# Seven-product SwiGLU with context: the w2 product behind two block products, A12 loaded twice, two block sums made by accumulating transfers

## The chip, the core and the metric

The kernel runs on one core of a Trainium2 chip. The metric is the device time of one execution in microseconds (us). A core has a matrix engine (TensorE, PE in the profile), a vector engine (VectorE, DVE), a scalar engine (ScalarE, ACT), GpSimd (POOL) and a queue that issues transfers (SyncE, SP). Matmuls read SBUF and write PSUM; weights and activations that don't fit in SBUF are fetched from device memory (HBM) by transfers (DMA).

## What is computed

A backbone of two layers over 512 latent tokens `x` and 256 context tokens `ctx`, width 1024. Each layer is half-step SwiGLU, token mixing, half-step SwiGLU; every sub-layer is normalised and modulated by shift, scale and gate vectors that a large matrix product (`w_ada`, 9 times 1024 columns per layer) makes of a conditioning vector. The context goes through the same weights, except for the last SwiGLU.

```python
def swiglu(x, w1, w3, w2):
    return (jax.nn.silu(x @ w1) * (x @ w3)) @ w2

def macaron_half(h, m, i, g, w1, w3, w2):
    y = swiglu(modulate(rms_norm(h, g), m[:, 3 * i], m[:, 3 * i + 1]), w1, w3, w2)
    return h + 0.5 * m[:, 3 * i + 2, None, :] * y
```

`w1` and `w3` have 2816 columns, 22 blocks of 128. Everything is float32.

## The kernel before, in words

Activations are kept transposed: `self.h` is eight tiles of 128 x 768 (256 context and 512 latent columns). A float32 product is made of three matmuls (`mm3`, L396 to L398): each operand is split into a high and a low part, the high part by ACT (L403, or L406 with a factor), the low part by a subtraction on DVE (L404, or L407), and high x high, high x low and low x high are summed in PSUM. So a block of weights passes through a tile `raw` (as loaded by SP, five such tiles) and a tile `w` (split, four such tiles), 128 x 1024 each: 512 KB.

Of the four SwiGLUs, the first of layer 0 is plain. The other three go through `ffn7`, which treats the hidden blocks in 11 pairs and saves one of eight block products: with the weights of a pair as blocks A11, A12, A21, A22 it makes seven products of sums of A blocks with sums of activation blocks. Two of these three carry the context too. In the trace of before, the first of them (the second SwiGLU of layer 0, **stage A** below) lies from 1045 to 1530 us, the other (the first SwiGLU of layer 1, **stage B**) from 1595 to 2080 us; the last SwiGLU of layer 1, for `x` alone, is the end of the program.

The first pair of an `ffn7` is plain (`first_pair`); `combine` makes the sums of activation blocks after it, and `pair(j, middle)` runs for each later pair. In `pair`, the products are B11 into PSUM bank Y, B21 into X, E into Y, t3 into X, t1 into Y, t4 into X, B22 into Y, each of 8 `mm3`, 24 matmuls of 384 columns. `snapshot` (L888) copies a bank to a tile `y` by ACT; `gated` (first line L894) adds a bank to such a copy on DVE and makes the gated hidden values of it. `middle()` is the w2 product of the pair before: for 8 blocks of rows of `h` and both streams, two hidden blocks into a bank B (6 matmuls of 512 columns for `x`, 6 of 256 for the context), and an accumulation into `h` on DVE (L905). It comes behind B11. The sums of weight blocks are three DVE additions of 128 x 1024, L973 (A21 + A22), L974 (A11 + A21) and L975 (A11 + the first), and L977 updates A12.

The modulation vectors are made beside all this: `self.mod_queue` holds pieces of work, each a load of a block of `w_ada` and two custom DVE instructions (L483), and `mods` says how many of them are taken behind which pair.

The order of instructions on each engine is not the order of this code: a list scheduler arranges it when the kernel is built, under the limits of the tiles (five `raw`, four `w`, 44 others).

Of the kernel before, what the change touches and what calls it, by code (L numbers as in the profile page):

```python
# [312 lines left out]
class Builder:  # L313
# [315 lines left out]
    def ffn(self, l, i, n, gate, nxt, streams=(X_COLS, C_COLS), begin=None, mods=0, split=None):  # L629

        nc = self.nc
        w13, w2 = self.a["w13"][l], self.a["w2"][l, i]
# [167 lines left out]

    def split_block(self, r, scale=None):
        w = self.mp.tile([128, 2, 1024], F32R, tag="w", name=self.name("w"), bufs=self.wslots)
        self.split_psum(w[:, 0], w[:, 1], r, scale)
        return w

    def ffn7(self, l, i, n, t, gate, nxt, streams=(X_COLS, C_COLS), split=None, late=None, mods=()):
# [12 lines left out]
        mp13, w2 = self.a["w13s"][2 * l + i - 1], self.a["w2"][l, i]  # L819
# [11 lines left out]
        def combine(k):  # L831

            u, v = t[k], t[k + 4]
            tensor = nc.vector.tensor_tensor
            tensor(out=u[:, n1], in0=u[:, n1], in1=u[:, n2], op=ALU.subtract)
            tensor(out=u[:, n2], in0=v[:, n2], in1=u[:, n2], op=ALU.subtract)
            tensor(out=v[:, n2], in0=u[:, n1], in1=v[:, n2], op=ALU.add)
            tensor(out=v[:, n1], in0=v[:, n2], in1=v[:, n1], op=ALU.subtract)
            c = slice(halves[0][0], halves[1][1])
            hi, lo = self.hl(T, "c")  # L840
            self.split_psum(hi[:, c], lo[:, c], v[:, c])
            tt[k, "t4"], tt[k, "E"] = ([p[:, q] for p in (hi, lo)] for q in (n1, n2))
            owned.append((hi, lo))
            if k % 2 == 0:
                box["t3"] = self.hl(2 * wd, "c")
                owned.append(box["t3"])
            tt[k, "t3"] = [p[:, k % 2 * wd:k % 2 * wd + wd] for p in box["t3"]]
            self.split_psum(*tt[k, "t3"], u[:, n2])
            self.free(t.pop(k + 4))

        def combine_rest():

            for k in range(4):
                tt[k, "t1"] = [p[:, n2] for p in n[k]]
                self.split_psum(*tt[k, "t1"], t[k][:, n1])
                self.free(t.pop(k))
# [41 lines left out]
        def down(fs, ws, d, cols):  # L898
# [3 lines left out]
            for x, f in enumerate(fs):  # L902
                self.mm3(ps[:, 0:c1 - c0], [ws[x][:, p, d * 128:d * 128 + 128] for p in range(2)],
                         (g[f][0][:, c0:c1], g[f][1][:, c0:c1]), x == 0, x == len(fs) - 1)
# [48 lines left out]
        def second(j):  # L953
            return [self.unit(w2[f]) for f in (2 * j, 2 * j + 1)]

        def pair(j, middle):
# [3 lines left out]
            Y, X = (self.ps("S", (j + x) % 2) for x in range(2))  # L960
            r11 = self.block(src[0, 0])
            product(Y, self.split_block(r11), "B11", True)
            middle()
            y0 = snapshot(Y, "y")
            gtiles(j)
            s = [self.m3(base="silu") for _ in range(2)]
            r12 = self.block(src[0, 1])
            product(X, self.split_block(r12), "B21", True)
            r21, r22, s1 = self.block(src[1, 0]), self.block(src[1, 1]), self.block(None)
            gated(s[0], n1, X, y0, 1.0)  # L970
            self.free(y0[0])
            parts(fs[0], s[0], n1)
            add(s1, r21, r22)  # L973
            add(r21, r11, r21)  # L974
            add(r11, s1, r11)  # L975
            product(Y, self.split_block(r11, -1.0), "E", False)
            add(r12, r11, r12)  # L977
            y1 = snapshot(Y, "y")
            product(X, self.split_block(r21), "t3", True)
            w0 = snapshot(X, "y")  # L980
            if j == 1:
                combine_rest()
            product(Y, self.split_block(s1), "t1", False)
            gated(s[1], n2, Y, w0, -1.0)
            self.free(w0[0])
            product(X, self.split_block(r22), "t4", False)
            if j == np_ - 1:
                self.free(owned)
# [3 lines left out]
            product(Y, self.split_block(r12), "B22", False)  # L992
            self.last_silu = nc.scalar.activation(s[0][:, n2], Y[:, 0:wd], AF.Silu)
# [6 lines left out]
        for k in range(4):  # L1000
            combine(k)
# [913 lines left out]
```

## Time and profile before

| what | value |
|---|---|
| median of 3 runs | 2764.53 us (2761.27 to 2767.53) |
| the profiled execution, own time | 2769.52 us |
| its span in the trace | 2767.7 us |
| granted TensorE clock, mean | 0.984 |
| PE, DVE, ACT, POOL busy | 96%, 74%, 39%, 10% of the span |
| mean share of the 16 DMA engines, q1 | 27.6% |

The profiled execution is 5.0 us longer than the median. An execution's own time is 1.8 us longer than its span, for what lies around it. The granted clock is the share of TensorE's full clock that the chip allowed; 0.50 means that matmuls started half as often.

### The profile page before, as it was taken

How to read it: one execution, taken by the hardware profiler on the slowest of the kernel's cores; microseconds unless marked ns; L12 is line 12 of the kernel's file. 1: busy time of each engine (PE TensorE's matmuls, PEld its weight loads, DVE VectorE, ACT ScalarE, POOL GpSimd, SP SyncE). 2: the span in 40 equal slices, each digit the busy share in tenths (PEclk: the TensorE clock that was granted, in tenths of full speed). 3: DMA queues.
4: the chain of work that ended last, by engine and by line, in shares of the span. 5: the costliest groups of instructions: out<-in, count | busy, mean ns of one | idle time of the engine just before them, and what ended most of it. 6: DMA issues, size and time to landing. Idle time of an engine off the chain costs nothing.

```text
span 2767.7 us, 40029 instructions
## 1 busy us (share of the span) xinstructions
PE 2658.0 (96%) x15788; PEld 2357.8 (85%) x15788; DVE 2046.8 (74%) x3551; ACT 1087.9 (39%) x1895; POOL 278.8 (10%) x370
## 2 busy tenths in 40 slices
PE   7999999999989998999999989999999989999999
PEld 5788888888867788999899879999998877888998
DVE  8986776655775559778676799887756675587886
ACT  4311211124665653233232632323335665544443
POOL 5100000001352210000000100000001352100000
PEclk8899999999989999999999999999999999999999
DMA  7542433211200013233222244443222210123322
GB/s 246 162 136 94 158 117 113 83 54 56 75 22 24 12 46 111 90 102 99 81 75 69 67 125 128 141 144 121 84 76 67 69 32 24 39 80 106 98 93 91
DMA packets 78673, 249.60 MB, mean 90 GB/s; under 512 B 8978, under 2 KB 10642, under 8 KB 78484
## 3 DMA queue, kind: packets, MB, share of 16 engines
q1 hardware_dynamic: 78484, 247.03, 27.6%
q8 instruction: 124, 2.03, 0.3%
q14 instruction: 65, 0.53, 0.1%
HBM read 244.90 MB, written 2.10 MB: 89 GB/s over the span
## 4 chain that ended last, share of the span: by engine, by line
PE 78%; DVE 14%; ACT 3%; issue 3%; DMA 2%; POOL 0%; SPq 0%; DVEq 0%; ACTq 0%; POOLq 0%
PE S L396 14%; PE S L398 13%; PE S L397 13%; PE B L397 10%; PE B L398 10%; PE B L396 10%; PE B L1424 3%; DVE w L404 2%; DVE junk L483 2%; PE B L1575 2%; DVE h L905 1%; DMA raw<-in_w13s 1%; DMA ada<-in_w_ada 1%; ACT w L403 1%; PE B L1543 1%
## 5 line engine op out<-in xcount | busy, mean ns | idle before, releaser
L403 ACT CAST w<-raw 128x1024 fp32r<-128x1024 f32 (+1 forms) x369 | 381.3, 1044 | 723.3 <-issue 330.0
L397 PE MATMUL S<-nlo,w 128*128 128x256 f32 (+2 forms) x1808 | 598.0, 331 | 9.4 <-DVE nlo L605 6.2
L396 PE MATMUL S<-nhi,w 128*128 128x256 f32 (+2 forms) x1808 | 590.0, 332 | 12.7 <-DVE silu L994 4.3
L398 PE MATMUL S<-nhi,w 128*128 128x256 f32 (+2 forms) x1808 | 596.4, 331 | 2.7 <-DVE w L404 2.5
L404 DVE TENSOR_TENSOR w<-raw,w 128x1024 fp32r<-128x1024 f32 (+1 forms) x369 | 449.2, 1229 | 95.3 <-ACT w L403 94.2
L397 PE MATMUL B<-glo,w 128*128 128x512 f32 (+1 forms) x1232 | 425.4, 346 | 5.6 <-DVE glo L870 5.6
L398 PE MATMUL B<-ghi,w 128*128 128x512 f32 (+1 forms) x1232 | 423.0, 346 | 3.1 <-DVE w L404 3.1
L396 PE MATMUL B<-ghi,w 128*128 128x512 f32 (+1 forms) x1232 | 416.2, 348 | 6.4 <-DVE h L905 2.7
L905 DVE SCALAR_TENSOR_TENSOR h<-B,g,h 128x512 f32<-128x512 f32 (+1 forms) x440 | 273.3, 642 | 145.5 <-PE B L398 144.7
L397 PEld LDWEIGHTS S<-nlo,w 128*128 128x128 f32 x1808 | 343.6, 190 | 33.8 <-DVE nlo L605 10.5
L396 PEld LDWEIGHTS S<-nhi,w 128*128 128x128 f32 x1808 | 341.4, 190 | 35.7 <-DVE silu L994 4.3
L398 PEld LDWEIGHTS S<-nhi,w 128*128 128x128 f32 x1808 | 344.2, 190 | 25.8 <-DVE w L404 6.9
L397 PEld LDWEIGHTS B<-glo,w 128*128 128x128 f32 x1232 | 232.0, 188 | 35.5 <-DVE glo L870 6.5
L396 PEld LDWEIGHTS B<-ghi,w 128*128 128x128 f32 x1232 | 229.8, 188 | 37.8 <-DVE h L905 5.1
L483 DVE CUSTOM_DVE_ANT_0 junk<-ada,bc,mpart 128x768 f32<-128x768 f32 x238 | 245.6, 1032 | 20.3 <-DMA ada<-in_w_ada 16.9
L398 PEld LDWEIGHTS B<-ghi,w 128*128 128x128 f32 x1232 | 231.7, 188 | 33.8 <-DVE w L404 3.8
L396 PE MATMUL S<-chi,w 128*128 128x384 f32 (+1 forms) x720 | 232.1, 323 | 13.5 <-ACT y L888 10.7
L398 PE MATMUL S<-chi,w 128*128 128x384 f32 (+1 forms) x720 | 229.1, 321 | 2.7 <-DVE w L404 2.1
L397 PE MATMUL S<-clo,w 128*128 128x384 f32 (+1 forms) x720 | 230.5, 321 | 0.0
L691 DVE SCALAR_TENSOR_TENSOR h<-B,g,h 128x256 f32<-128x256 f32 (+1 forms) x176 | 103.8, 615 | 101.6 <-PE B L398 101.6
L532 POOL TENSOR_TENSOR sq<-sq,sq 128x512 f32<-128x512 f32 (+1 forms) x38 | 42.2, 1112 | 1159.3 <-ACT sq L528 1158.1
L888 ACT COPY y<-S 128x768 f32<-128x768 f32 (+1 forms) x90 | 65.5, 728 | 237.7 <-PE S L398 130.9
(267 smaller groups left out, 4413.6 us busy)
## 6 DMA issues: line engine op xcount, KB each, us to landing
raw<-in_w SPq DMA_DIRECT2D x132, 512.0 KB, 3.6
raw<-in_w13s SPq DMA_DIRECT2D x132, 512.0 KB, 3.8
ada<-in_w_ada SPq DMA_DIRECT2D x171, 384.0 KB, 4.0
raw<-in_w_out SPq DMA_DIRECT2D x16, 512.0 KB, 4.3
ada<-in_ada SPq DMA_DIRECT2D x16, 384.0 KB, 6.4
raw<-in_w_in_t SPq DMA_DIRECT2D x10, 512.0 KB, 3.5
raw<-in_dftx SPq DMA_DIRECT2D x8, 512.0 KB, 3.5
ada<-in_ada SPq DMA_DIRECT2D x8, 256.0 KB, 5.2
```

Source lines behind the costliest of these rows:

```text
L396: mm(out, lhs[0], rhs[0], start=start, stop=False, skip_group_check=more)
L397: mm(out, lhs[0], rhs[1], start=False, stop=False, skip_group_check=more)
L398: mm(out, lhs[1], rhs[0], start=False, stop=stop, skip_group_check=more)
L403: nc.scalar.copy(hi, src)
L404: nc.vector.tensor_sub(lo, src, hi.bitcast(F32))
L483: nc.vector.tensor_tensor_reduce(out=self.junk[:, 0:w.shape[1]], in0=w, in1=v, scale=1.0, scalar=init, op0=ALU.mult, op1=ALU.add, accum_ou ...
L532: (nc.vector if part else nc.gpsimd).tensor_add(st[key], st[key], t)
L691: nc.vector.scalar_tensor_tensor(out=self.h[d][:, c0:c1], in0=ps[:, 0:c1 - c0], scalar=gate()[:, d, s:s + 1], in1=self.h[d][:, c0:c1], op0 ...
L888: nc.scalar.copy(v, both(bank))
L905: nc.vector.scalar_tensor_tensor(out=self.h[d][:, c0:c1], in0=ps[:, 0:c1 - c0], scalar=gate()[:, d, s:s + 1], in1=self.h[d][:, c0:c1], op0 ...
L1424: mm(outs[y], lhs[y], rhs[y], start=start, stop=stop)
L1575: nc.tensor.transpose(pt[:, x * 256 + i * 128:x * 256 + i * 128 + 128], Ps[i, y][:, tok(kp * 2 + x)], self.ident)
```

## The change

For the two SwiGLUs with context (not for the last one), five things are different.

1. `middle()` stands behind B11, B21 and the first `gated`, and no longer between B11 and B21.
2. w2 is packed anew: a half-unit holds both hidden blocks of a pair for 512 columns, and each half is loaded and split when its first use comes.
3. A21 + A22 and A11 + A21 are made by transfers (`block_sum`): SP loads the first block into a `raw` tile, and a second transfer, issued by POOL (L805), reads the other block from HBM and adds it to that tile. The two DVE additions are gone. As A11 + A21 no longer overwrites A21 nor uses the loaded A11, and since A12 and A22 are fetched where they are used, A12 is loaded twice. In 20 pairs this is 2 more SP loads and 2 POOL transfers each: SP's transfers go from 548 to 588 rows, POOL's rows from 325 to 365, DVE's from 3552 to 3517. PE has 15035 rows in both.
4. `combine` runs in three parts within the first of these pairs, ahead of the product that needs each, and no longer whole ahead of it.
5. The pieces of the modulation begin two pairs later.

The core of the diff:

```diff
+    def block_sum(self, *srcs):
+        r = self.block(srcs[0])
+        for src in srcs[1:]:
+            self.nc.gpsimd.dma_start(out=r, in_=src, accum_op=ALU.add)
+        return r
...
         def pair(j, middle):
...
+            first = combine if j == 1 else lambda name: None
             r11 = self.block(src[0, 0])
             product(Y, self.split_block(r11), "B11", True)
-            middle()
+            if x_only:
+                middle()
             y0 = snapshot(Y, "y")
...
             r12 = self.block(src[0, 1])
             product(X, self.split_block(r12), "B21", True)
...
             gated(s[0], n1, X, y0, 1.0)
             self.free(y0[0])
+            if not x_only:
+                middle()
+                gtiles(j)
             parts(fs[0], s[0], n1)
-            add(s1, r21, r22)
-            add(r21, r11, r21)
+            if x_only:
...
+            else:
+                s1, s3 = self.block_sum(src[1, 0], src[1, 1]), self.block_sum(src[0, 0], src[1, 0])
+            first("E")
             add(r11, s1, r11)
             product(Y, self.split_block(r11, -1.0), "E", False)
-            add(r12, r11, r12)
+            if x_only:
+                add(r12, r11, r12)
+            else:
+                r12 = self.block(src[0, 1])
             y1 = snapshot(Y, "y")
-            product(X, self.split_block(r21), "t3", True)
+            first("t4")
+            first("t3")
+            product(X, self.split_block(s3), "t3", True)
             w0 = snapshot(X, "y")
             product(Y, self.split_block(s1), "t1", False)
+            if not x_only:
+                add(r12, r11, r12)
             gated(s[1], n2, Y, w0, -1.0)
-            product(X, self.split_block(r22), "t4", False)
+            product(X, self.split_block(r22 if x_only else self.block(src[1, 1])), "t4", False)
             gated(s[1], n1, X, y1, -1.0)
...
             product(Y, self.split_block(r12), "B22", False)
...
-                self.ffn7(l, 1, n, before.t, self.gate(l, 8, 2, 0.5), nxt, mods=(1,) * 8)
+                self.ffn7(l, 1, n, before.t, self.gate(l, 8, 2, 0.5), nxt, mods=(0,) * 2 + (1,) * 8)
...
-    o["w2"] = np.stack([a[f"w2_ffn{i}"].reshape(L, NF, 128, D) for i in (1, 2)], 1)
+    o["w2"] = a["w2_ffn1"].reshape(L, NF, 128, D)[0:1]
+    w2 = np.stack([a["w2_ffn2"][0], a["w2_ffn1"][1], a["w2_ffn2"][1]])
+    o["w2s"] = w2.reshape(3, NF // 2, 2, 128, 2, 512).transpose(0, 1, 4, 3, 2, 5).reshape(3, NF // 2, 2, 128, 1024)
```

In the changed file the additions are at L998 (A11 + s1) and L1011 (A12), `gated` begins at L903, the accumulation into `h` is at L915.

How the instructions of DVE stand around the two last `gated` of a pair of stage A. Before (`y_1901` with bank S_1852 is the last `gated` of one pair, L973 and L974 the sums of the next pair's weights):

```order
L896 SCALAR_TENSOR_TENSOR silu_1892_10309<-y_1899_10380,silu_1892_10309 128x384
L894 TENSOR_TENSOR y_1901_10409<-S_1852_10107,y_1901_10409 128x768
L483 ISA junk_1762_9411,mpart_1937_10693<-ada_1929_10673,bc_1761_9402,sml_77 128x256
L483 ISA mpart_1937_10693 128x1
L404 TENSOR_TENSOR w_1912_10542<-raw_1911_10540,w_1912_10542 128x1024
L483 ISA junk_1762_9411,mT_78<-ada_1931_10675,bc_1760_9401,mpart_1937_10693 128x768
L483 ISA mT_78 128x1
L896 SCALAR_TENSOR_TENSOR silu_1892_10309<-y_1901_10409,silu_1892_10309 128x384
L973 TENSOR_TENSOR raw_1950_10740<-raw_1948_10736,raw_1949_10738 128x1024
```

In the change, the same place (`w_1994` is the split A12 for B22, `raw_2038` the sum A21 + A22 of the next pair, made by the accumulating transfer; `y_1990` with S_1941 is `gated` behind t1, `y_1988` with S_1942 that behind t4):

```order
L404 TENSOR_TENSOR w_1994_11235<-raw_1987_11137,w_1994_11235 128x1024
L915 SCALAR_TENSOR_TENSOR h7_76<-B_1968_11055,g_1798_9735,h7_76 128x512
L915 SCALAR_TENSOR_TENSOR h7_76<-B_1969_11063,g_1798_9735,h7_76 128x256
L404 TENSOR_TENSOR w_1998_11270<-raw_1997_11268,w_1998_11270 128x1024
L998 TENSOR_TENSOR raw_1997_11268<-raw_2038_11503,raw_1997_11268 128x1024
L903 TENSOR_TENSOR y_1990_11168<-S_1941_10866,y_1990_11168 128x768
L903 TENSOR_TENSOR y_1988_11139<-S_1942_10867,y_1988_11139 128x768
L404 TENSOR_TENSOR w_2001_11301<-raw_2000_11299,w_2001_11301 128x1024
```

Before, both `gated` additions stand ahead of the next pair's sums. In the change, the sum L998, which reads what the accumulating transfer leaves, stands ahead of both. It stands so in 6 consecutive pairs of stage A; in stage B it stands behind both (5 pairs) or between them (4).

How the instructions of PE stand at the end of a pair. Before (S_1958 takes t1 with `w_2008`, later B22; S_2011 takes B11 of the next pair):

```order
L397 MATMUL S_1958_10901<-nlo_1720_9186,w_2008_11205 128x384
L398 MATMUL S_1958_10901<-nhi_1719_9185,w_2008_11205 128x384
L396 MATMUL B_2020_11347<-ghi_1993_11098,w_2016_11331 128x256
L397 MATMUL B_2020_11347<-glo_1994_11099,w_2016_11331 128x256
L396 MATMUL B_2022_11363<-ghi_1993_11098,w_2016_11331 128x256
L397 MATMUL B_2022_11363<-glo_1994_11099,w_2016_11331 128x256
L396 MATMUL S_2011_11298<-nhi_1713_9179,w_2014_11302 128x384
L397 MATMUL S_2011_11298<-nlo_1714_9180,w_2014_11302 128x384
```

In the change (S_1941 takes t1 with `w_1991` and then B22 with `w_1994`, S_1942 takes t4 with `w_1993`):

```order
L397 MATMUL S_1941_10866<-nlo_1720_9186,w_1991_11170 128x384
L398 MATMUL S_1941_10866<-nhi_1719_9185,w_1991_11170 128x384
L397 MATMUL S_1942_10867<-clo_1829_9904,w_1993_11203 128x384
L398 MATMUL S_1942_10867<-chi_1828_9903,w_1993_11203 128x384
L396 MATMUL S_1941_10866<-nhi_1721_9187,w_1994_11235 128x384
L397 MATMUL S_1941_10866<-nlo_1722_9188,w_1994_11235 128x384
L398 MATMUL S_1941_10866<-nhi_1721_9187,w_1994_11235 128x384
```

B22 overwrites the bank that `gated` reads. Before, some 30 matmuls (four of w2, 24 of the next pair's B11, two more of w2) stand between t1's last and B22's first; in the change two matmuls do. Ahead of these, from t3's last matmul on, PE has two groups of w2 (6 matmuls of 512 columns and 6 of 256), 22 matmuls of t4 and the 24 of t1.

How SP's transfers stand in such a pair of the change (`raw_1992` is A22; `raw_1997` and `raw_2000` are A11 and A12 of the next pair; `raw_2005` and `raw_2015` the halves of w2; `raw_2038` and `raw_2039` the first blocks of the two sums; `raw_2041` A12 again):

```order
L798 DMA raw_1992_11201<-in_w13s 128x1024
L491 DMA ada_1973_11074<-in_w_ada 128x768
L798 DMA raw_1997_11268<-in_w13s 128x1024
L798 DMA raw_2000_11299<-in_w13s 128x1024
L491 DMA ada_2024_11471<-in_w_ada 128x768
L388 DMA raw_2005_11334<-in_w2s 128x1024
L388 DMA raw_2015_11403<-in_w2s 128x1024
L798 DMA raw_2038_11503<-in_w13s 128x1024
L798 DMA raw_2039_11506<-in_w13s 128x1024
L798 DMA raw_2041_11537<-in_w13s 128x1024
```

Before there were four loads of `in_w13s` in a pair, all plain; now the load of `raw_2038` waits until the tile of `raw_1987` is free, which is when DVE has split it (`w_1994` above), and POOL's accumulating transfer into `raw_2038` waits until that load has landed. The split of `w_1994` waits for t3's last matmul, whose weight tile it takes over.

## Rows read from the trace of the kernel before

**Rows 1.** The page's first part: busy time, share of the span, instructions.

```profile
PE 2658.0 (96%) x15788; PEld 2357.8 (85%) x15788; DVE 2046.8 (74%) x3551; ACT 1087.9 (39%) x1895; POOL 278.8 (10%) x370
```

**Rows 2.** Windows: stretch, length, PE, PEld, DVE, ACT, POOL busy, clock, DMA share, GB/s.

```profile
1045.00:1115.00 70.00, 65.30 (x359) 61.30 (x358) 66.80 (x122) 24.31 (x33) 0.00 (x0) 0.95 0.36 110
1115.00:1360.00 245.00, 234.52 (x1294) 221.31 (x1293) 190.90 (x313) 74.05 (x95) 0.00 (x0) 0.98 0.30 95
...
1595.00:1690.00 95.00, 81.58 (x443) 75.30 (x442) 92.35 (x178) 27.21 (x37) 0.00 (x0) 0.95 0.37 117
1690.00:2080.00 390.00, 388.46 (x2202) 368.70 (x2201) 307.23 (x486) 126.29 (x162) 3.98 (x8) 1.00 0.37 117
```

**Rows 3.** Waits of PE, 1045 to 1360: us in total, times, longest.

```profile
PE B L397 <- DVE glo L870: 4.9, 3, 2.4
PE S L396 <- DVE silu L994: 2.6, 3, 0.9
...
PE S L396 <- ACT y L888: 1.5, 2, 0.9
```

**Rows 4.** Waits of PE, 1595 to 1690.

```profile
PE S L396 <- ACT y L888: 8.0, 3, 5.3
...
PE B L398 <- DVE w L404: 1.2, 1, 1.2
PE S L396 <- DVE silu L925: 1.0, 1, 1.0
```

**Rows 5.** Timeline in the opening of stage A: start, duration, instruction, idle before.

```profile
1104.99 1.06 ACT L406 ACTIVATE w<-raw 128x1024 fp32r<-128x1024 f32 x1 [1.54 <-DVE raw L975]
...
1106.10 0.66 PE L396 MATMUL S<-chi,w 128*128 128x384 f32 x1 [1.99 <-ACT w L406]
```

**Rows 6.** Windows behind three stops of PE, columns as in rows 2.

```profile
1106.20:1109.50 3.30, 3.30 (x11) 3.30 (x12) 3.30 (x7) 0.51 (x1) 0.00 (x0) 0.50 0.41 119
1157.40:1160.70 3.30, 3.30 (x12) 3.30 (x12) 3.30 (x8) 0.71 (x2) 0.00 (x0) 0.50 0.00 0
...
1631.70:1635.20 3.50, 3.48 (x11) 3.48 (x12) 3.46 (x8) 0.00 (x0) 0.00 (x0) 0.50 0.81 271
```

**Rows 7.** Groups by line and form, 1045 to 1530: count | busy us, mean ns | idle.

```profile
L404 DVE TENSOR_TENSOR w<-raw,w 128x1024 fp32r<-128x1024 f32 x78 | 94.7, 1222 | 22.6 <-ACT w L403 22.5
L403 ACT CAST w<-raw 128x1024 fp32r<-128x1024 f32 x79 | 82.5, 1048 | 185.7 <-PE S L398 163.3 <-issue 22.4
...
L483 DVE CUSTOM_DVE_ANT_0 junk<-ada,bc,mpart 128x768 f32<-128x768 f32 x48 | 48.8, 1016 | 5.5 <-DMA ada<-in_w_ada 5.2
...
L894 DVE TENSOR_TENSOR y<-S,y 128x768 f32<-128x768 f32 x30 | 28.6, 955 | 11.5 <-PE S L398 11.5
...
L975 DVE TENSOR_TENSOR raw<-raw,raw 128x1024 f32<-128x1024 f32 x10 | 12.2, 1221 | 0.0
```

**Rows 8.** Timeline of PE at full clock: matmuls of 384, 512, 256 columns.

```profile
1119.73 0.34 PE L396 MATMUL S<-chi,w 128*128 128x384 f32 x1
...
1121.85 0.34 PE L396 MATMUL S<-chi,w 128*128 128x384 f32 x1
1122.02 0.40 PE L396 MATMUL B<-ghi,w 128*128 128x512 f32 x1
...
1124.56 0.39 PE L398 MATMUL B<-ghi,w 128*128 128x512 f32 x1
1124.79 0.28 PE L396 MATMUL B<-ghi,w 128*128 128x256 f32 x1
...
1126.11 0.28 PE L398 MATMUL B<-ghi,w 128*128 128x256 f32 x1
```

**Rows 9.** DMA issues of the whole span: count, KB each, median us to landing.

```profile
raw<-in_w13s SPq DMA_DIRECT2D x132, 512.0 KB, 3.8
...
cst<-in_consts SPq DMA_DIRECT2D x1, 64.0 KB, 2.0
```

**Rows 10.** Groups by line and form, 0 to 110 us, where POOL computes.

```profile
L483 DVE CUSTOM_DVE_ANT_0 junk<-ada,bc,mpart 128x768 f32<-128x768 f32 x21 | 25.3, 1204 | 0.2
```

More of the change, by code (lines that the diff above doesn't have):

```diff
@@ L631, in ffn @@
         nc = self.nc
[L632 removed]
+        w13, w2 = self.a["w13"][l], self.a["w2"][l]
         off = {X_COLS: 512, C_COLS: 256}
@@ L829, in ffn7, with parts_of, combine @@
         tt, box, owned = {}, {}, []
-        def combine(k):
-            u, v = t[k], t[k + 4]
+        def parts_of(name, k, parts, src):
+            tt[k, name] = parts
+            self.split_psum(*parts, src)
+        def combine(name):
             tensor = nc.vector.tensor_tensor
[L835 to L849, printed above, removed]
@@ L851, in combine_rest @@
-        def combine_rest():
-            for k in range(4):
-                tt[k, "t1"] = [p[:, n2] for p in n[k]]
-                self.split_psum(*tt[k, "t1"], t[k][:, n1])
-                self.free(t.pop(k))
+            for k in range(4):
+                u, v = t[k], t[k + 4]
+                if name == "E":
+                    tensor(out=u[:, n1], in0=u[:, n1], in1=u[:, n2], op=ALU.subtract)
+                    tensor(out=u[:, n2], in0=v[:, n2], in1=u[:, n2], op=ALU.subtract)
+                    tensor(out=v[:, n2], in0=u[:, n1], in1=v[:, n2], op=ALU.add)
+                    tensor(out=v[:, n1], in0=v[:, n2], in1=v[:, n1], op=ALU.subtract)
+                    box[k] = self.hl(T, "c")
+                    owned.append(box[k])
+                    parts_of("E", k, [p[:, n2] for p in box[k]], v[:, n2])
+                elif name == "t4":
+                    parts_of("t4", k, [p[:, n1] for p in box[k]], v[:, n1])
+                    self.free(v)
+                else:
+                    parts_of("t1", k, [p[:, n2] for p in n[k]], u[:, n1])
+                    if k % 2 == 0:
+                        box["t3"] = self.hl(2 * wd, "c")
+                        owned.append(box["t3"])
+                    parts_of("t3", k, [p[:, k % 2 * wd:k % 2 * wd + wd] for p in box["t3"]], u[:, n2])
+                    self.free(u)
@@ L902, in down @@
             for x, f in enumerate(fs):
-                self.mm3(ps[:, 0:c1 - c0], [ws[x][:, p, d * 128:d * 128 + 128] for p in range(2)],
+                o = x * 512 + d % 4 * 128
+                self.mm3(ps[:, 0:c1 - c0], [ws(d // 4)[:, p, o:o + 128] for p in range(2)],
                          (g[f][0][:, c0:c1], g[f][1][:, c0:c1]), x == 0, x == len(fs) - 1)
@@ L953, in second @@
         def second(j):
-            return [self.unit(w2[f]) for f in (2 * j, 2 * j + 1)]
+            ws = {}
+            return lambda half: ws[half] if half in ws else ws.setdefault(half, self.unit(w2[j, half]))
         def pair(j, middle):
@@ L992, in pair @@
             product(Y, self.split_block(r12), "B22", False)
+            if j == np_ - 1:
+                self.free(owned)
             self.last_silu = nc.scalar.activation(s[0][:, n2], Y[:, 0:wd], AF.Silu)
@@ L999, in ffn7 @@
         first_pair()
-        for k in range(4):
-            combine(k)
         def middle(j):
@@ L1761, in build @@
                 tabs = []
-                self.ffn7(l, 0, n, t, self.gate(l, 2, 2, 0.5), nxt, late=lambda: tabs.extend(self.rope_tables(l)), mods=(2,) * 8)
+                self.ffn7(l, 0, n, t, self.gate(l, 2, 2, 0.5), nxt, late=lambda: tabs.extend(self.rope_tables(l)), mods=(0,) * 2 + (2,) * 8)
             else:
```

17 lines of the change are left out of this document (9 added, 8 removed).

## The prediction

> **What bounds the kernel now.** I read the page's first part, then windows by stage, then PE's waits in the stages that the change touches, then the timeline at the longest of them. PE is busy 96% of the span [rows 1], so the end is set by its matmuls and by its stops. The change leaves the matmuls as they are; it can only remove stops, or add some. Windows tell how much there is to remove [rows 2]: PE's idle time is 70.0 − 65.3 = 4.7 us in the opening of stage A, 245 − 234.5 = 10.5 us in the five or so pairs behind it, 95 − 81.6 = 13.4 us in the opening of stage B and 390 − 388.5 = 1.5 us in the rest of it. In these windows DVE is busy 95%, 78%, 97% and 79%, the transfers 30 to 37%. PE waits there for DVE's results, or for ACT's that wait for DVE's: for the low parts `glo` and the last product `silu` of a pair in stage A [rows 3], for the snapshot `y` in the opening of stage B, where a stop lasts 5.3 us [rows 4]. One stop shows the chain whole: PE waits 1.99 us for a split by ACT, which waited 1.54 us for the sum L975 on DVE [rows 5]. Behind such a stop the granted clock falls: 0.50 for 3.3 us in three rows [rows 6], with one more stretch like the first, two like the second. That is 6 stretches by 3.3 us by a half, 9.9 us.
>
> **The sum, part by part.** The profiled execution took 2769.52 us, 5.0 over the median of 2764.53; I make the sum as a difference to it and take the same difference from the median.
>
> *Removed.* The w2 product needs the low parts `glo`; put behind B21 it comes 24 matmuls later, 24 x 0.177 = 4.2 us (twelve steps in 2.12 us) [rows 8], more than the longest wait for `glo`, 2.4 us [rows 3]. Two additions of 1.22 us leave DVE in each pair [rows 7], the sums of activations no longer stand together in the opening, and the modulation, 1.02 us and more for each piece [rows 7], leaves the openings. So I take all idle time of rows 2, 30.1 us, and the 9.9 us of clock as gone, but for 1.2 + 1.0 us in the first pair of stage B, which the change doesn't touch [rows 4]: 30.1 + 9.9 − 2.2 = **37.8 us** removed.
>
> *Moved and at no price.* The modulation pieces that start two pairs later fall into pairs in which DVE has time (79% busy, less 2.4 us of additions in 47 us per pair); if that cover were gone they would return as waits for `glo`, 10.5 us at most. The repacked w2 has the same bytes, splits and matmuls. The 40 further SP loads and 40 POOL transfers are 80 x 512 KB; the engines of the transfers are 30 to 37% busy there [rows 2], so bandwidth isn't the price, delay is.
>
> *Added: a chain ahead of B22.* In 6 pairs of stage A the changed order puts L998, which reads the accumulated sum, ahead of both `gated` additions, and B22 may not overwrite its bank before these. DVE works in order, so B22 waits for the transfer. From t3's last matmul: cast 1.05, subtraction 1.22 [rows 7] (the tile is free), SP's plain load 3.8 [rows 9], the accumulating transfer x, L998 1.22, `gated` 0.95 [rows 7]: 8.2 + x, with some 0.1 between engines 8.3 + x. PE has in that time 6 matmuls of 512 (0.231 each) and 6 of 256 (0.12) [rows 8], 2.1 us; a wait for a snapshot that the new order also brings, since `y_1990` takes over a tile that the last w2 matmul reads, 0.9 us as such waits were [rows 3]; then 48 matmuls by 0.177, 8.5 us: 11.4 in all. So the stop is x − 3.1 us, with 1.65 us of clock behind it if it is a stop like those of rows 6.
>
> *The price x.* No row shows an accumulating transfer. Bounded below by a plain one of the same size, 3.8, since it moves the same bytes and reads the old ones besides, so a gain is excluded; above by two of them, 7.5. Between the two I take the part that moves bytes twice, and the rest once: 64 KB took 2.0 and 512 KB 3.8 [rows 9], so 448 KB cost 1.8 and 512 KB some 1.9 (an estimate from these two rows): x = 3.7 + 1.9 = 5.6. The Trainium skill (DMA: Bandwidth & Descriptors, section Anatomy of one DMA — SWDGE (gpsimd) path) fits a transfer issued by GpSimd with 2.0 us and bytes at 436 KB per us: 3.2 us for 512 KB and, with the bytes counted twice, an estimate of 4.4; the sum below would then be −14.7. That is a fit for plain transfers, and no run here shows one from GpSimd; I stay with the rows.
>
> At x = 5.6 each of the 6 pairs costs 0.9 + 2.5 + 1.65 = 5.05 us: **30.3 us**. In stage B the sum doesn't stand ahead of the first `gated`, so that price is nought there; if that cover is gone it is up to 9 pairs by 1.5 us.
>
> *Sum.* −37.8 + 30.3 = −7.5 us against the profiled execution, so 2757.0 against the median. At x = 3.7 a pair costs 0.9 + 0.6 = 1.5 us, with no fall of the clock, since the stops of 0.9 us [rows 3] show none: 9 us, −28.8, 2735.7. At x = 7.5 it is 0.9 + 4.4 + 1.65 = 6.95: 41.7 us, +3.9, and +17.4 with stage B's 13.5: 2781.9. Sum and price are equal at 0.9 + (x − 3.1) + 1.65 = 6.3, so x = 6.85.
>
> **The rivals.**
>
> *An accumulating transfer is hardly slower than a plain one.* For it: the transfer engines are free two thirds of the time [rows 2], and bytes move fast once started, 1.8 us for 448 KB [rows 9]. Against it: the data must be read from two places and added. With x of 3.7 to 4.5 the pairs cost 9 to 6 x 3.95 = 23.7 us: 2736 to 2750; I name 2741.
>
> *The accumulating transfer stands at the head of DVE's queue (the other side).* With x of 7 or more L998 holds up DVE in stage A: behind it wait both `gated`, B22, and then the parts of the pair that w2 needs, and the sum of the next pair. It decides from x = 6.85. At x = 9 a pair costs 0.9 + 5.9 + 1.65 = 8.45, 50.7 us, so +12.9, and with stage B's 13.5 it is +26.4: 2791. For it: nothing in this trace excludes it, and the path has never been used here; the chain has only 11.4 us of cover. Against it: the two loads whose time it would take are only 3.8 each.
>
> *GpSimd prepares the transfer late.* A DVE operation slows when GpSimd computes beside it: the modulation's L483 takes 1.20 us there and 1.02 elsewhere [rows 10, 7], so the two engines share something. If the issue of the transfer stood back behind one DVE addition of 1.22, x would be 6.8 and the change worth nothing: −37.8 + 6 x 6.25 = −0.3, 2764. The Trainium skill (SBUF — State Buffer, section SBUF: two separate sides, the trap "DVE blocks DMA") says that transfers issued from GpSimd wait for their descriptors while DVE is in a mode that uses both ports; it counts additions of two tensors as harmless to descriptors, by inference. No row here shows a transfer from GpSimd.
>
> *The openings stay.* The change may not do what it says: the sums of activations are as many instructions as before, and DVE is busy 95 and 97% in the openings [rows 2]. If half of their idle time and clock returned, (4.7 + 1.65 + 13.4 + 3.3 − 2.2) / 2 = 10.4 us, the time is 2757.0 + 10.4 = 2767.
>
> **How the numbers follow.** Forecast (x of 4.6 to 6.3, openings mostly gone) 0.38, 2757.0. Cheap transfer 0.18, 2741. Dear transfer 0.32, 2782 to 2791 where stage B pays too. Late GpSimd 0.05, 2764; openings stay 0.07, 2767. About 0.2%, 5.5 us, is what a measurement of this kernel can tell from no change. Faster by more than that: 0.29 of the forecast (its cases with x under 5.9), all of the cheap transfer, and 0.01 of the openings with such a transfer: 0.48. Slower by more: 0.30 of the dear transfer (x over 7.8, or a lower one with a price in stage B) and 0.04 of the openings with x at the forecast's upper end: 0.34. Within: the remaining 0.18. The range: from the lower bound of x, 2736, to the dear transfer with stage B, 2791, and leaves out what lies beyond x = 9 and a plain-load price without any residue. Of its width the price x makes nearly all. The forecast's own range is 2741 to 2762.
>
> **What will show it right or wrong.** Right: the accumulating transfers land 4.6 to 6.3 us after their issue in the list of transfers; PE's idle time in the opening of each stage is under 3 us; in stage A there are six stops of some 2.5 us at the first matmul of B22, put down to DVE's `gated` L903, with L998 just ahead of it and its own wait on the transfer, each with a window of clock 0.50 behind; six waits of some 0.9 us for the snapshot; and no waits for `glo`. Wrong: the same stops in stage B, which I hold at nought; a landing time outside 3.7 to 7.5; L998 waiting for SP's load rather than for POOL's transfer; waits for `glo` that remain; or no stop at B22 at all, which would mean that the plain load starts earlier than by the chain above.

## The result and the profile after

The changed kernel took 2794.62 us (median of 5 runs, 2780.5 to 2798.77), the kernel before 2764.53 in the same series: ratio 1.0098, 95% interval 1.0069 to 1.0128. It is slower by 30 us, where 7.5 us faster was forecast. The profiled execution is its fastest, 2780.5 us with a span of 2778.7, so the trace shows 11.0 us of the 30. It is read first for these 11. Two executions among those below lie far from all others (8984.82 us of the kernel before, 3450.19 us of the kernel with the addition on GpSimd) and are left out of the ratios.

The first part of the changed kernel's page, which answers to [rows 1]:

```profile
PE 2659.5 (96%) x15788; PEld 2361.3 (85%) x15788; DVE 2006.1 (72%) x3523; ACT 1091.7 (39%) x1907; POOL 319.7 (12%) x410
```

DVE lost 41 us of work, POOL took on as much, PE's work is the same. Windows of the changed kernel by stage, columns as in [rows 2], then one behind a stop of PE, and one at the end of stage B:

```profile
1045.00:1115.00 70.00, 69.40 (x394) 65.61 (x394) 50.37 (x75) 27.78 (x41) 2.48 (x3) 1.00 0.42 113
1115.00:1360.00 245.00, 230.72 (x1289) 217.86 (x1288) 173.54 (x287) 73.43 (x93) 8.69 (x10) 0.99 0.49 139
1595.00:1690.00 95.00, 92.30 (x545) 86.38 (x544) 72.71 (x116) 41.42 (x68) 2.62 (x3) 1.00 0.34 100
1690.00:2080.00 390.00, 384.26 (x2172) 364.23 (x2171) 308.19 (x536) 125.06 (x157) 13.94 (x16) 1.00 0.55 167
1287.90:1291.20 3.30, 2.85 (x9) 2.85 (x10) 3.30 (x4) 1.05 (x2) 0.00 (x0) 0.50 0.00 0
2085.00:2120.00 35.00, 28.81 (x142) 22.52 (x141) 32.41 (x58) 15.79 (x27) 17.57 (x16) 0.95 0.28 99
```

Both openings are nearly without idle time: 0.6 us of 70 instead of 4.7, 2.7 of 95 instead of 13.4. The pairs behind them lose more than before: 14.3 us instead of 10.5 in stage A, 5.7 instead of 1.5 in stage B. And PE now idles 6 us of 35 at the end of stage B, against 1.2 us of 35 at the same place before (2081 to 2116 in its trace). PE's waits in stage A say for what:

```profile
PE S L396 <- DVE y L903: 19.8, 8, 3.0
PE S L396 <- ACT y L897: 4.6, 6, 0.8
```

These are the two waits of the forecast: `gated` ahead of B22 (seven stops of 2.4 to 3.0 us and one of 0.7), and the snapshot. One of the stops in the timeline, DVE's instructions first, then POOL's and PE's of the same pair:

```profile
1275.13 1.23 DVE L404 TENSOR_TENSOR w<-raw,w 128x1024 fp32r<-128x1024 f32 x1 [1.09 <-ACT w L403]
...
1286.20 1.23 DVE L998 TENSOR_TENSOR raw<-raw,raw 128x1024 f32<-128x1024 f32 x1 [6.52 <-DMA raw<-in_w13s]
1287.35 1.82 DVE L903 TENSOR_TENSOR y<-S,y 128x768 f32<-128x768 f32 x2
```

```profile
1280.62 0.86 POOL L805 DMA_DIRECT2D raw<-in_w13s  x1 [37.17 <-DMA raw<-in_w13s]
```

```profile
1288.35 0.69 PE L396 MATMUL S<-nhi,w 128*128 128x384 f32 x1 [2.84 <-DVE y L903]
```

DVE splits A12 at 1275.13; SP's load goes out as that ends and lands before 1280.62, where POOL issues the accumulating transfer; L998 starts 5.58 us later, having kept DVE idle for 6.52 us; both `gated` follow it, and PE stands 2.84 us. The transfers' list gives the price x:

```profile
raw<-in_w13s SPq DMA_DIRECT2D x172, 512.0 KB, 3.6
...
raw<-in_w13s POOLq DMA_DIRECT2D x40, 512.0 KB, 5.7
```

For the experiments one measure is used throughout: the lost time of PE in a profiled execution, which is its idle time and half of the time at a granted clock of 0.50 (1.2 GHz instead of 2.4). It is cut where DVE makes the last gated product of a pair (L994 before, L1022 after), to half a us. In us:

| stretch | before | change | place alone | place, late pieces | place, parts | place, parts, late pieces | change, sum on GpSimd | change, plain second load |
|---|---|---|---|---|---|---|---|---|
| A, pair 1 | 4.0 | 0.6 | 0.6 | 0.0 | 1.1 | 0.6 | 0.6 | 0.6 |
| A, pairs 2 to 10 | 17.5 | 34.8 | 10.8 | 11.0 | 10.8 | 10.4 | 10.7 | 11.1 |
| A, end | 1.4 | 6.9 | 2.1 | 10.8 | 2.1 | 12.8 | 7.0 | 5.3 |
| B, pair 1 | 15.5 | 0.6 | 0.8 | 0.0 | 11.7 | 0.6 | 0.6 | 0.6 |
| B, pairs 2 to 10 | 2.4 | 5.7 | 6.7 | 4.7 | 4.8 | 3.7 | 9.2 | 0.5 |
| B, end | 1.3 | 7.9 | 5.6 | 10.7 | 3.9 | 10.1 | 11.8 | 6.2 |
| sum | 42.1 | 56.5 | 26.6 | 37.2 | 34.4 | 38.2 | 39.9 | 24.3 |
| median, us | 2764.5 to 2767.3 | 2794.6, 2788.9 | 2755.7 | 2768.5 | 2774.6 | 2765.8 | 2769.2 | 2752.5 |

The last six columns are experiments of the next section ("place, parts, late pieces" is the one with both sums on DVE). Change less before: +17 in A's pairs, −18 in the two openings, +12 at the two ends, +3 in B's pairs: +14.4. The span shows +11.0, and so does the lost time of the whole trace (154.1 us before, 165.3 after): the other 3 us were gained outside these stretches. The medians in the last row don't follow the sums closely: the column "place, parts" lost 7.7 us less than before in its profile and has a median 8 us higher.

### The profile page after: what moved, and what is told of

Read it like the earlier page. It is cut to its first block, busy times and chain, and to the rows that moved or that the text cites. A ratio compares the mean times of both kernels' runs of the same rounds, so it can differ in the third digit from the quotient of the medians.

```text
span 2778.7 us, 40239 instructions
## 1 busy us (share of the span) xinstructions
PE 2659.5 (96%) x15788; PEld 2361.3 (85%) x15788; DVE 2006.1 (72%) x3523; ACT 1091.7 (39%) x1907; POOL 319.7 (12%) x410
## 4 chain that ended last, share of the span: by engine, by line
PE 76%; DVE 11%; DMA 6%; issue 3%; ACT 3%; POOL 1%; SPq 0%; DVEq 0%; POOLq 0%; ACTq 0%
PE S L396 13%; PE S L398 13%; PE S L397 13%; PE B L397 10%; PE B L398 10%; PE B L396 10%; DMA raw<-in_w13s 4%; PE B L1450 3%; DMA ada<-in_w_ada 2%; DVE w L404 2%; DVE junk L483 2%; PE B L1601 2%; DVE h L915 1%; ACT w L403 1%; PE B L1569 1%
## 5 line engine op out<-in xcount | busy, mean ns | idle before, releaser
L397 PE MATMUL S<-nlo,w 128*128 128x256 f32 (+2 forms) x1808 | 600.5, 333 | 10.6 <-DVE nlo L605 8.2
L396 PE MATMUL B<-ghi,w 128*128 128x512 f32 (+1 forms) x1232 | 422.1, 349 | 14.3 <-DVE h L915 9.9
L397 PEld LDWEIGHTS S<-nlo,w 128*128 128x128 f32 x1808 | 346.5, 192 | 33.3 <-DVE nlo L605 11.1
L915 DVE SCALAR_TENSOR_TENSOR h<-B,g,h 128x512 f32<-128x512 f32 (+1 forms) x440 | 270.5, 640 | 97.4 <-PE B L398 96.0
L483 DVE CUSTOM_DVE_ANT_0 junk<-ada,bc,mpart 128x768 f32<-128x768 f32 x238 | 247.9, 1042 | 28.9 <-DMA ada<-in_w_ada 25.5
L396 PEld LDWEIGHTS S<-chi,w 128*128 128x128 f32 x720 | 135.4, 188 | 9.7 <-ACT y L897 6.1
L805 POOL DMA_DIRECT2D raw<-in_w13s x40 | 35.0, 874 | 937.4 <-DMA raw<-in_w13s 370.7
```

What stands on the lines that cost most here:

```text
L396: mm(out, lhs[0], rhs[0], start=start, stop=False, skip_group_check=more)
L397: mm(out, lhs[0], rhs[1], start=False, stop=False, skip_group_check=more)
L483: nc.vector.tensor_tensor_reduce(out=self.junk[:, 0:w.shape[1]], in0=w, in1=v, scale=1.0, scalar=init, op0=ALU.mult, op1=ALU.add, accum_ou ...
L805: self.nc.gpsimd.dma_start(out=r, in_=src, accum_op=ALU.add)
L915: nc.vector.scalar_tensor_tensor(out=self.h[d][:, c0:c1], in0=ps[:, 0:c1 - c0], scalar=gate()[:, d, s:s + 1], in1=self.h[d][:, c0:c1], op0 ...
```

## The experiments

Theories after the result: the loss is (1) the waiting addition at the head of DVE's queue, or the transfer as such, and (2) the modulation pieces that run over the stage ends. Rivals: the new place of the w2 product, or the extra 42 MB of loads. The scheduler arranges the instructions anew for every edit. Only the first kernel below and the plain second load have the change's order on every engine; in the others the time of an edit includes what the new arrangement brought. The kernels were measured in four series, each beside the kernel before, whose median lay between 2765.9 and 2767.3 us in them.

**The same kernel again.** No edit.

> The changed kernel unaltered, for a second profile and for the spread of its runs. Theory (the accumulating transfer at the head of DVE's queue in stage A, and modulation pieces that run over the end of both stages): 2780 to 2800 us, the same seven stops of 2.4 to 3.0 us ahead of B22 in stage A, put down to gated (L903). If an execution is near 2795 rather than 2780, the theory expects the difference in longer stops at these same places and in the clock behind them. Rival (the extra 42 MB slow other loads at large): the difference is spread over waits for other loads.

2788.87 us (2781.28 to 2792.1), ratio 1.0078 [1.0064, 1.0091]. The profile (2782.23 us) repeats the first one to a tenth: gated 19.7 us in 8 waits, the snapshot 4.6 in 6. So the stops are the same in two profiles; whether the slower executions near 2790 have longer ones was not to be seen, since both profiles fell on executions at the low end. The clock is less regular than the stops: in both profiles a stretch at 0.50 stands behind five of the seven only, and stops of 2.39 and 2.85 us in the first have none (clock lost 10.2 and 8.5 us).

**Modulation pieces early.**

```diff
-... mods=(0,) * 2 + (2,) * 8)
+... mods=(2,) * 8)
...
-... mods=(0,) * 2 + (1,) * 8)
+... mods=(1,) * 8)
```

> The changed kernel with the modulation pieces started where they were before (no two empty pairs). Theory: the idle time at the ends of stage A and B (6.2 + 6.2 us in the profile, against 1.0 + 1.3 before) goes, some 10 us with its clock: 10 us under the changed kernel, 2770 to 2788; the stops ahead of B22 stay. Rival (the shift is what cleared the opening of stage B): the opening's waits return, 13 us, and the time is not lower than the changed kernel's.

2804.78 us, ratio 1.0137 [1.0123, 1.0150]: a miss. The ends became shorter, as expected (lost time 2.1 and 5.5 us instead of 6.9 and 7.9), but the opening of stage B (8.3 instead of 0.6) and the pairs (38 and 12 instead of 34.8 and 5.7) took back more. The rival holds for this kernel: what cleared the opening of stage B was the shift. Its stops ahead of B22 are like the change's, 2.1 to 3.1 us, and here all seven have a stretch at 0.50 behind them, 13.7 us of clock.

**Both sums on DVE.** Four plain loads in a pair and three additions, the rest as changed.

```diff
-                s1, s3 = self.block_sum(src[1, 0], src[1, 1]), self.block_sum(src[0, 0], src[1, 0])
+            r21, r22, s1 = self.block(src[1, 0]), self.block(src[1, 1]), self.block(None)
+            add(s1, r21, r22)
+            add(r21, r11, r21)
...
```

> The changed kernel with the sums of weight blocks by DVE additions from four plain loads, as before; the w2 product, the parts of combine and the modulation pieces stay as changed. Theory (the accumulating transfer is the loss): the stops ahead of B22 and their clock go, 30 to 34 us: 2750 to 2765 us. Rival (the new place of the w2 product or the late modulation is the loss): 2780 us or more, and waits for DVE at other places.

2765.76 us, ratio 1.0001 [0.9992, 1.0010]: 23.1 under the changed kernel (less than the 30 to 34 that it should have given), and exactly before's time. So in this kernel the transfers cost 23 us, and all the rest of the change together brings nothing. Its openings are clear, and A's pairs lose 10.4 us instead of before's 17.5, which together is 25 us less; the two stage ends take 20 us of it back (12.8 and 10.1 us instead of 1.4 and 1.3).

**The waiting addition on GpSimd.**

```diff
-            add(r11, s1, r11)
+            (add if x_only else nc.gpsimd.tensor_add)(r11, s1, r11)
```

> The changed kernel with only the addition that waits for the accumulating transfer (A11 + s1) on GpSimd instead of DVE; the transfers stay. Theory (order on DVE: the waiting addition holds up gated): the stops ahead of B22 go although the transfers are as slow as they were, 2750 to 2770 us. Rival (the data simply come too late, whoever adds): PE waits as long for the split of E, 2785 us or more.

2769.18 us (2768.57 without the execution of 3450 us), ratio 1.0011 [1.0001, 1.0020]. The transfers are as slow as they were (5.9 us), and the waits for `gated` ahead of B22 have gone from stage A, whose longest sum of waits is now

```profile
PE B L396 <- DVE h L915: 8.9, 8, 2.1
```

So some 20 of the 23.1 us go when the instruction that waits for late data no longer stands in front of others on DVE. The edit also takes 1.22 us of work in each pair off DVE, but that isn't the cause: with all three additions on DVE, in the kernel above, there were no such stops either.

**The new place of the w2 product alone.** Sums on DVE, pieces early, `combine` whole (all its parts ahead of the first of these pairs). It is called "place alone" here, though w2's new packing comes with it, and `combine` splits its sums in smaller steps and makes t1's earlier than the kernel before did.

```diff
-            first = combine if j == 1 else lambda name: None
+            first = lambda name: None
...
         first_pair()
+        for name in ("E", "t4", "t3"):
+            combine(name)
...
```

> The kernel before with the new place and packing of the w2 product alone: sums of weight blocks by DVE, combine whole ahead of the first of these pairs, modulation pieces as early as before. Theory (the openings are crowded by DVE's work: combine and the pieces, and the place of the w2 product clears only the waits for the low parts): the waits for the low parts and silu in the pairs of stage A go, some 10 us, the openings keep theirs, 13 us and more: 2755 to 2768 us. Rival (the place itself clears the openings): the openings' idle time falls under 3 us and the time to 2745 or less. Other rival (the place itself costs): over 2772.

2755.73 us, ratio 0.9954 [0.9941, 0.9967]: **faster than both kernels**, by 11.3 us than before in the same series. The time falls into the theory's range by luck, since the openings are nearly the rival's: lost time 0.6 and 0.8 us up to the end of pair 1, with DVE as busy there as before. A stop of 2.7 us for the snapshot has moved into stage B's pair 2, so the opening's window still has 3.5 us of idle time. The window of stage B's opening, against [rows 2]:

```profile
1595.00:1690.00 95.00, 91.55 (x510) 86.01 (x509) 92.31 (x174) 30.41 (x41) 0.00 (x0) 0.98 0.43 131
```

What it doesn't bring is in the pairs of stage A. The waits for the low parts are gone; in their place stand

```profile
PE S L396 <- ACT y L897: 6.0, 8, 0.8
PE S L396 <- DVE y L903: 4.9, 7, 0.7
```

**A plain second load.** The second transfer of a sum is not accumulating, so this kernel leaves the sums of weight blocks out and shows times alone.

```diff
-            self.nc.gpsimd.dma_start(out=r, in_=src, accum_op=ALU.add)
+            self.nc.gpsimd.dma_start(out=r, in_=src)
```

> The changed kernel with the second transfer of each sum a plain load from GpSimd instead of an accumulating one, in the same order on every engine; the second block overwrites the first, so the sums of weight blocks are left out. Theory (the addition in the transfer is a second read, 1.9 us of the 5.7): it lands in 3.7 to 4.2 us, the seven stops fall from 2.7 to about 1 us and lose their clock, 18 us in all: 2770 to 2778. Rival (what costs is that GpSimd issues it: descriptors, not the addition): it lands in 5 us or more and the time stays at 2782 to 2792.

2752.53 us, ratio 0.9945 [0.9934, 0.9957], 36 under the changed kernel, twice what was expected. The transfers' list, and PE's waits in stage A:

```profile
raw<-in_w13s POOLq DMA_DIRECT2D x40, 512.0 KB, 3.9
```

```profile
PE S L396 <- DVE y L903: 6.5, 6, 1.3
PE S L396 <- ACT y L897: 4.6, 6, 0.8
```

With the same order on every engine, 1.8 us less of landing take 19.8 − 6.5 = 13.3 us from these waits, and with them all the clock lost in these pairs (10.2 us). So late data and the order on DVE cost together: this run takes away the lateness and keeps the order, the run with the addition on GpSimd takes away the order and keeps the lateness, and the stops shrink or go in both. That GpSimd issues the transfer costs little (3.9 against 3.5 from SP in this run); the addition does. The stops are 1.1 us each, the clock stays at 1.00 in these pairs, and the sum x − 3.1 gives 0.8. The kernel moves the same 42 MB more as the change and is 14.5 us faster than before, so the bytes alone are not the loss. The two profiled executions differ by 25.8 of the 36 us.

**The w2 product at its old place, the transfers kept.**

```diff
-            if x_only:
-                middle()
+            middle()
...
-            if not x_only:
-                middle()
-                gtiles(j)
```

> The changed kernel with the w2 product at its old place behind B11; the accumulating transfers, the parts of combine and the late modulation pieces stay. In its order the waiting addition stands ahead of only one gated, and 24 matmuls of t4 lie between t1 and B22. Theory: 4.2 us of matmuls cover the stops of 2.8, so they go, but waits for the low parts return in the pairs, 2 us each: 2770 to 2785 us. Rival (the transfers cost wherever the w2 product stands): 2788 us or more.

2764.21 us, ratio 0.9989 [0.9979, 0.9999]. A miss on the good side: lost time in A's pairs 2 to 10 is 10.4 us, with one stop of 4.9 us in four waits for `gated`. So the transfers with the w2 product at its old place (and `combine` in parts, pieces late) don't cost, nor does the place alone. Together they do, as the new place brings t1's end within two matmuls of B22.

**One sum by transfer.** A11 + A21 by transfer, A21 + A22 by DVE in place.

```diff
-                s1, s3 = self.block_sum(src[1, 0], src[1, 1]), self.block_sum(src[0, 0], src[1, 0])
+                s1, r22 = self.block(src[1, 0]), self.block(src[1, 1])
+                add(s1, s1, r22)
+                s3 = self.block_sum(src[0, 0], src[1, 0])
...
```

> The changed kernel with only A11 + A21 by the accumulating transfer, which no addition waits for (its splits read it), and A21 + A22 by DVE in place; A12 and A22 are loaded once. Theory (what costs is DVE standing behind the transfer, not the transfer): no stops ahead of B22, one addition less on DVE than with both sums there: 2755 to 2766 us. Rival (the transfer comes too late for t3 too): waits for the split of t3's weights, 2775 us or more.

2765.16 us, ratio 0.9993 [0.9985, 1.0002]. In stage A's pairs 4 to 9 PE idles 1.3 us, though a transfer lands 5.8 us after its issue: no DVE addition stands behind it. Stage B pays it back: waits for `h` of 6.3 us and for the split of a weight of 4.1 in two stops. Ahead of the longer one, 2.67 us, ACT's split itself waits 5.94 us for the transfer. So the rival's wait is there too, in few pairs: without any addition behind it the transfer can be late for its own reader.

**Place alone, with that sum in stage A alone.** The edit above with `if l or x_only:` for the plain way.

> The kernel before with the new place of the w2 product, and in stage A alone A11 + A21 by the accumulating transfer (A21 + A22 by DVE in place); the modulation pieces early, combine whole. Theory (a transfer that no addition of DVE stands behind only takes work from DVE): the waits for gated and for snapshots in stage A, 7.4 us of idle time in its pairs 4 to 9 with the new place alone, fall to some 1.5: 2744 to 2752 us. Rival (the transfer delays the split of t3's weights once the pieces of the modulation are early): 2756 us or more.

2768.40 us, ratio 1.0008 [0.9999, 1.0017]: a miss, 13 us above the place alone, with the rival's wait in A's pair 1: a split stands 5.09 us behind the transfer, and PE stops for 2.93. A's pairs 4 to 9 kept their 8 us. And the opening of stage B, whose code is that of the place alone, lost 8.9 us instead of 0.8, with a snapshot wait of 5.1 us as before the change: DVE's instructions stand there in another order. Why they do is not known. So a clear opening, with the same code, can also be lost to the arrangement, and single differences of some 10 us between the kernels here may be of that kind.

**Combine in parts; then the pieces late with combine whole.** The first is the place alone with `first = combine if j == 1 ...` as changed, the second the place alone with the two empty pairs.

> The new place of the w2 product with DVE sums and early modulation pieces, and combine in parts as changed. It differs from the kernel with late pieces and DVE sums (2765.8) in the pieces alone, and from the new place alone (2755.7) in combine alone. Theory (late pieces cost at the stage ends what they save in the openings, and the openings are clear without them): 2754 to 2758 us, so the late pieces cost 8 to 10. Rival (combine in parts costs, the pieces are worth nothing): 2763 to 2768.

> The new place of the w2 product with DVE sums and combine whole (2755.7 with early modulation pieces), and the pieces two pairs later as changed. It completes the square of combine (whole, in parts: 2755.7, 2774.6 early) and pieces (early, late: 2774.6, 2765.8 in parts). Theory (late pieces cost at both stage ends whatever combine does, and clear an opening only where combine in parts has crowded it): 2762 to 2768 us, the stage ends some 10 us longer, the openings as with early pieces. Rival (late pieces are a gain by themselves, combine in parts is the whole loss): 2750 us or less.

2774.57 us, ratio 1.0028 [1.0018, 1.0038], a miss, beyond the rival's range too; and 2768.51 us, ratio 1.0002 [0.9991, 1.0014], at the upper end of the theory. With the new place of w2 and DVE sums in all four:

| median, us | pieces early | pieces late |
|---|---|---|
| combine whole | 2755.7 | 2768.5 |
| combine in parts | 2774.6 | 2765.8 |

The kernel with combine in parts is 18.9 us slower when the pieces are early; its profile shows 12 us of that in the span and 7.8 in the lost time of the table. In its opening of stage B (11.7 us lost instead of 0.8) PE waits for the split of an activation sum, which in parts is made just ahead of its product:

```profile
PE S L396 <- ACT chi L403: 4.0, 2, 3.4
```

The kernel with late pieces as well is free of that wait and 8.8 us faster; with combine whole, where nothing is to be cleared, late pieces cost 12.8 us. The waits at the end of stage B with the place alone, then with late pieces:

```profile
PE B L396 <- ACT ghi L878: 1.7, 1, 1.7
PE B L396 <- DVE h L915: 1.1, 2, 0.8
```

```profile
PE B L396 <- DVE h L915: 3.4, 3, 1.6
PE B L396 <- ACT ghi L878: 2.3, 1, 2.3
```

A group of DVE in the second, at that same end, fits this (columns as in [rows 7]):

```profile
L483 DVE CUSTOM_DVE_ANT_0 junk<-ada,bc,mpart 128x768 f32<-128x768 f32 x6 | 8.0, 1339 | 0.4 <-DMA ada<-in_w_ada 0.4
```

Six long pieces stand between the last accumulations into `h`; with the place alone none do. They also take 1.34 us there on average instead of 1.02 [rows 7]. The mean mixes two cases: three of them run while GpSimd squares for the next norm (L532) and take 1.55 to 1.88 us, the other three take 1.01 to 1.02. [Rows 10] had a mean of 1.20 where GpSimd computes.

**The waiting addition on GpSimd with early pieces.**

> The changed kernel with the waiting addition on GpSimd (2769.2 with late pieces) and the modulation pieces early. Theory (late pieces cost 8 to 10 at the stage ends): 2758 to 2763 us. Rival (early pieces crowd the openings when the sums are transfers, as they did in the changed kernel, +15): 2775 us or more.

2773.02 us, ratio 1.0028 [1.0018, 1.0039]: a miss by 10 us, close to the rival. It has combine in parts, and it waits more again (5.8 us for `nlo` in stage A's first, plain pair; 5.2 us lost in stage B's opening; 10.6 us in 12 waits for `h` over all of stage B), as with the other kernels that join parts and early pieces.

## Why the prediction was wrong

2757.0 us was forecast and 2794.6 measured, 37.6 us more. The miss has two halves. The profiles hold the first: the profiled execution took 2780.5 us, where the sum made it 2769.5 − 7.5 = 2762.0, so 18.5 us are terms of the sum. In lost time, over the stretches of the table:

| term | forecast, us | profile of the change, us |
|---|---|---|
| removed | −37.8 | −32.3 |
| added ahead of B22 | +30.3 | +34.6 |
| moved and at no price | 0 | +12.1 |
| together | −7.5 | +14.4 (span +11.0) |

(Removed: the openings and pairs lost 39.4 us before and 41.7 after, of which 34.6 are the added chain.)

*"The same difference from the median": this step failed.* It is the second half of the miss, 19.1 us, and the prediction gives no reason for it. The profiled execution of before is 5.0 us above its median, that of the change 14.1 us below. Where the slower executions of the change lose their time no profile shows.

*"Moved and at no price": this step failed, and is the largest error among the terms.* I named the cover for the late pieces, DVE's free time in the middle pairs, and gave 10.5 us at most for its loss, as waits for `glo`, which is the wrong place. The pieces run past the last pair, where DVE is needed for the accumulations into `h`: 5.5 and 6.6 us more lost time at the two ends in the profile of the change, 12.8 us of time in the square above where combine is whole. Combine in parts had no price at all in the sum; the kernel with it is 18.9 us slower with early pieces, though only part of that is in its profile.

*"Removed": short by 5.5 us, and its grounds don't hold.* It took "all idle time of rows 2" as gone. The openings went as forecast: 4.0 and 15.5 us of lost time became 0.6 each, and A's pairs have little left beside the chain. But B's pairs lose 5.7 us instead of 2.4, in waits for `h`. Without the transfers the gain in A's pairs is small: 10.4 to 10.8 us remain with the sums on DVE, since the waits for the low parts are replaced by waits for the snapshot and for `gated`, 0.7 to 0.8 us in almost every pair. And the place alone has clear openings with early pieces and combine whole: the two parts of the change that I credited with them were not needed there, and a mere rearrangement of the same code lost stage B's again.

*In medians* the parts were +22.8 us for the change of the second series, 2788.9, with before at 2766: the new place −10.3 (place alone), combine in parts and late pieces +10.0 (sums on DVE, less place alone), the transfers +23.1 (the change again, less sums on DVE). These add up by construction, along one path from before to the change; by another path the prices differ, as the transfers cost nothing at the old place. The forecast had −37.8 for the first two and +30.3 for the third.

*The price x: right.* 5.6 was forecast, 5.7 measured (5.3 to 8.8), and the part that it gave to the second passage of the bytes, 1.9, was measured as 1.8. Its sum is a little loose: from its own rows 448 KB in 1.8 us make 2.1 for 512 KB, and with 3.8 for the plain load x would be 5.9. The fit that it took from the Trainium skill (DMA: Bandwidth & Descriptors, section Anatomy of one DMA — SWDGE (gpsimd) path) gave an estimate of 4.4 with the bytes counted twice, and 3.2 for a plain transfer; the traces disagree, with 5.7 and 3.9.

*The chain ahead of B22: right in kind and nearly in size.* Forecast were 6 stops of 2.5 us, 6 snapshot waits of 0.9 and 6 x 1.65 us of clock, 30.3. The profile has 19.8 us of waits for `gated` (7 stops of 2.4 to 3.0, one of 0.7), six snapshot waits of 0.77 and 10.2 us of clock, 34.6 in all. The seventh stop is a pair in which the addition stands ahead of one `gated` only; the count from the order looked for both. That each stop would have its stretch at 0.50 did not come true: two of the seven have none, and one has two. In stage B no such stop exceeds 0.5 us, as forecast.

*The rivals.* The one on the other side, the accumulating transfer at the head of DVE's queue, is what the profile shows, but at x = 5.7, below the 6.85 that I gave it to decide: the point was set by a removal that was too large and by late pieces at no price. GpSimd preparing the transfer late falls as the usual case: the median is 5.7 and the shortest landing 5.3, and 3.9 when it is plain. "The openings stay" falls in the change as it is.

*What stays open.* The profile explains +11 us, the median +30 in the first series and +23 in the second. In the first series the slower executions have a granted clock of 0.979 to 0.980, the profiled one 0.983; 0.0035 of 2790 us is 10 us of the 14 between them. In the second series this doesn't hold throughout: two executions near 2789 us have 0.982 and 0.983, like the two near 2782. That it hangs on the transfers' landing the plain second load shows: in the same order it takes 36 us from the median, 10 more than between the profiles, and its executions run from 2751.5 to 2754.7 only. By which stops is open. A stretch at 0.50 behind more of them is one possibility, since the profiles differ in that (five stops of seven twice, all seven with early pieces, in the slowest of that kernel's four executions). It would give 1.7 us for each stop, and it is not shown.

## What to carry to other kernels

A transfer that replaces an addition is cheap or dear by what stands behind its reader: here nearly the same landing time (5.7 and 5.9 us) cost 23 us with DVE's queue behind it and 3 with the reader on another engine. Before a wait is booked as removed, look for what is late next in that pair, and book it; before work is booked as hidden, look at the stretch where it must end, not at the one where it begins. Before a difference in a profile is carried over to the median, see where the profiled execution lies among the others. Test the parts of a change apart: one part of this one, the new place of the w2 product with its packing, ran 11 us faster than before, and the others gave it away. And where a scheduler arranges every kernel anew, trust most the experiment that keeps the order.

## What the runs showed that was not expected

- Adding in the transfer costs 1.8 us for 512 KB (5.7 against 3.9 from the same queue), and GpSimd is busy 0.87 us with the issue, 0.53 with a plain one.
- A stop of 2.84 us has a clock of 0.50 for 3.4 us behind it, one of 2.85 us in the next pair has none, and stops of 1.1 us with the plain second load lost no clock at all: 1.8 us of landing were worth 23.7 us of lost time in nine pairs, of which 10.2 are clock.
- At the end of a stage a modulation operation (L483, 128x768) took 1.55 to 1.88 us beside a multiplication on GpSimd and 1.01 to 1.02 without, three times each.
- The same code in stage B's opening lost 0.8 us in one kernel and 8.9 in another, in another order of DVE's instructions.
